# Gate and up products of a SwiGLU with the tokens stationary, and six weight sections as seven half-size products with part of their weight sums made by DMAs that add

## Chip, cores and metric

One NeuronCore of a Trainium2 chip runs one transformer-like block on 256 tokens of width 1024, in float32. The metric is the device time of one execution in microseconds (us). Engines: TensorE (PE; its weight loads are PEld), VectorE (DVE), ScalarE (ACT), GpSimd (POOL), and SyncE (SP), which only issues transfers here.

## What is computed

```python
x = x + 0.5 * rmsnorm(swiglu(rmsnorm(x, g1), W_gate1, W_up1, W_down1), p1)   # D = 1024, F = 4096
h = rmsnorm(x, gm)
q, k, v, f, u, v_s, a_A, a_B = split(h @ W_in)                               # seven sections of 1024 columns, f of 8
o_A = forgetting_attention(q, k, v, f)                                       # 8 heads of 128
o_B = gelu(u) * (W_s @ layernorm(gelu(v_s)) + b)
x = x + rmsnorm((sigmoid(a_A) * o_A + sigmoid(a_B) * o_B) @ W_out, pm)
x = x + 0.5 * rmsnorm(swiglu(rmsnorm(x, g2), W_gate2, W_up2, W_down2), p2)

def swiglu(h, w_gate, w_up, w_down):
    return (silu(h @ w_gate) * (h @ w_up)) @ w_down
```

## The kernel before, in words

Every large product runs in float32r, in three passes: an operand is cut into `hi`, its leading bits, and `lo = x - hi`; the result is hi·hi + hi·lo + lo·hi. `split` (L77) makes both parts: ACT copies `hi` (L78) and DVE subtracts (L79). The weights are split when they have come from HBM: `load` (L90) brings 1 MiB into one of 3 raw buffers from SP's queue, `piece` (L97) splits 1024 of its 2048 columns into one of 11 pairs of buffers (`wts`). The tokens are two tiles of 128; their normalised, transposed and split form stands in `xT`.

The two SwiGLUs (`ffn`, L220) go over 32 F tiles of 128 hidden columns. `gate_up` (L232) makes gate and up of one F tile with the weights stationary and the tokens moving (`wide`, L189): per 128 rows of the contraction a product of 512 columns with `hi` (L194) and one of 256 with `lo` (L195). The result comes out transposed already, as the down product needs it: `wide_sum` (L197) adds its halves, `swiglu` (L212) applies silu, multiplies and splits it into `hT`. `down` (L265) then adds this F tile into four PSUM banks, six products of 512 columns per token tile (L274). The down products of the last 10 F tiles wait for token tile 1 until tile 0 is done (`DEFER`), and two of these come after tile 0 has been put into xT (`KEEP`). The second SwiGLU starts with 4 F tiles by token tile, tokens stationary (`gate_up_of`, L240, products of 256 columns, L250), since tile 1 is not normalised yet; their results are turned by PE transposes (L260).

The mixer takes 1024 columns at a time with the tokens stationary: `proj` (L316) does 512 columns of one token tile, three products (L321) per 128 rows. `section` (L327) does both token tiles with each weight, `section_by_tile` (L341) one tile and then the other. Small work on PE is put off by some of these steps (`later` and `tick`, L118, L121). The norms are made by ACT (squares, L139), POOL (root, L144, L146) and DVE (L164, L182, L186); `to_xT` (L154) transposes on PE (L158) and splits.

The program is written without engine orders except where `in_order` (L81) sets them. The order on each engine is fixed when the program is built, by what is expected to be ready first and then by the order written; a buffer is given to the next user when its last reader is done.

Of the kernel before, what the change touches and what calls it, by code (L numbers as in the profile page):

```python
# [34 lines left out]
DEFER = 10          # last F tiles whose down product waits for token tile 1 until token tile 0 is done  # L35
KEEP = 2            # of these, the ones that come after token tile 0 is put into xT
LEAD = 4            # F tiles of the second SwiGLU that are done by token tile
WARM = 14           # idle products before the first data are there
FORGET, SCORES, TURN = 5, 3, 3  # chunks of other work before these steps (see later)
# [3 lines left out]
def block(ctx: ExitStack, tc: tile.TileContext, a: dict, out: bass.AP):  # L43
    nc = tc.nc
    const = ctx.enter_context(tc.tile_pool(name="const", bufs=1))
    raws = ctx.enter_context(tc.tile_pool(name="raws", bufs=3))
    wts = ctx.enter_context(tc.tile_pool(name="wts", bufs=11))
    gains = ctx.enter_context(tc.tile_pool(name="gains", bufs=2))
    mid = ctx.enter_context(tc.tile_pool(name="mid", bufs=12))
    big = ctx.enter_context(tc.tile_pool(name="big", bufs=3))  # L50
    small = ctx.enter_context(tc.tile_pool(name="small", bufs=4))
# [29 lines left out]
    def in_order(instructions):  # L81
        """Each engine takes its instructions of the list in the list's order."""
# [14 lines left out]
    def piece(raw, j, name, trace=None):  # L97
        r = raw[:, j * 1024:(j + 1) * 1024]
        hi = wts.tile([P, 1024], F32R, tag="hi", name=f"hi_{name}_{j}")
        lo = wts.tile([P, 1024], F32R, tag="lo", name=f"lo_{name}_{j}")  # L100
        done = split(hi, lo, r)
        if trace is not None:
            trace.extend(done)
        return hi, lo

    def unit(src, name):
        """1 MiB of weights, split into two pieces of 1024 columns."""
        raw = load(src, name)
        return [piece(raw, j, name) for j in range(2)]
# [577 lines left out]
```

## Time and profile before

| | us |
|---|---|
| median of 3 runs | 766.69 (766.54 to 766.77) |
| span of the profiled execution | 766.7 |
| PE busy | 755.1 |
| DVE busy | 486.4 |
| ACT busy | 413.2 |
| POOL busy | 17.4 |
| read from HBM | 140.02 MB, 184 GB/s over the span |

The span runs from the first to the last instruction of one execution. PE's products are pipelined, so that the duration of one overlaps the next; how fast they follow each other is read from the starts in the timeline. Idle time of an engine is put down to what released it.

### The profile page before, as it was taken

The page shows a single profiled execution, that of the slowest core. Times are in us where ns is not written, and L with a number is a line of the kernel's source. Part 1 is how long each engine was busy: PE and PEld are TensorE (multiplying, and loading weights), DVE is VectorE, ACT ScalarE, POOL GpSimd, SP SyncE. Part 2 cuts the span into 40 slices and gives each one's busy share as a digit, 9 for nine tenths or more (in the row PEclk, how much of TensorE's full clock was granted, in tenths as well). Part 3 has the DMA queues.
Part 4 walks back from the last instruction along what each step waited for, and adds up shares of the span by engine and source line. Part 5 has one row for each costly group of instructions (what it writes and reads, how often), then busy time and mean ns, then how long its engine had stood idle before and what let it go on. Part 6 is the DMA issues. An engine that isn't in the chain of part 4 may idle for free.

```text
span 766.7 us, 10137 instructions
## 1 busy us (share of the span) xinstructions
PE 755.1 (98%) x3974; PEld 641.4 (84%) x3974; DVE 486.4 (63%) x731; ACT 413.2 (54%) x655; POOL 17.4 (2%) x32
## 2 busy tenths in 40 slices
PE   7999999999999999999999999999999999999996
PEld 4888888888888878888888888898888888888885
DVE  5885665666566586755486646875666566565652
ACT  4865555554545585754544434754555555554441
POOL 1000000000000020000010000200000000000000
PEclk8999999999999999999999999999999999999999
DMA  7885455555444366633346725555455545544401
GB/s 287 309 316 222 169 215 180 205 171 215 165 165 143 136 219 221 236 136 140 115 160 196 273 84 216 196 219 217 165 194 193 205 177 194 191 167 163 165 1 55
DMA packets 21983, 141.72 MB, mean 185 GB/s; under 512 B 3184, under 2 KB 3440, under 8 KB 5680
## 3 DMA queue, kind: packets, MB, share of 16 engines
q1 hardware_dynamic: 21936, 141.08, 51.0%
q8 instruction: 31, 0.51, 0.3%
q14 instruction: 16, 0.13, 0.1%
HBM read 140.02 MB, written 1.05 MB: 184 GB/s over the span
## 4 chain that ended last, share of the span: by engine, by line
PE 97%; DMA 1%; ACT 0%; DVE 0%; POOL 0%; issue 0%; SPq 0%; DVEq 0%; POOLq 0%; ACTq 0%
PE y L274 22%; PE g L194 15%; PE u L194 14%; PE u L195 8%; PE g L195 7%; PE qk L194 4%; PE gu L250 3%; PE v L321 3%; PE ga L321 3%; PE sv L321 3%; PE wo L321 3%; PE gb L321 3%; PE u L321 3%; PE qk L195 2%; DMA g_ffn_pre_g<-in_ffn_pre_g 1%; PE tp_f L158 1%
## 5 line engine op out<-in xcount | busy, mean ns | idle before, releaser
L79 DVE TENSOR_TENSOR lo_g<-raw_g,hi_g 128x1024 fp32r<-128x1024 f32 x128 | 155.9, 1224 | 88.0 <-ACT hi_g L78 87.8
L78 ACT CAST hi_g<-raw_g 128x1024 fp32r<-128x1024 f32 x128 | 133.3, 1049 | 73.8 <-PE y L274 60.0
L194 PE MATMUL u<-xT,hi_g 128*128 128x512 f32 x480 | 171.4, 394 | 0.0
L194 PE MATMUL g<-xT,hi_g 128*128 128x512 f32 x480 | 171.2, 395 | 0.0
L274 PE MATMUL y<-hi_d,hT 128*128 128x512 f32 x512 | 148.7, 392 | 0.0
L195 PE MATMUL u<-xT,lo_g 128*128 128x256 f32 x480 | 135.9, 283 | 0.0
L195 PE MATMUL g<-xT,lo_g 128*128 128x256 f32 x480 | 135.0, 281 | 0.0
L79 DVE TENSOR_TENSOR lo_d<-raw_d,hi_d 128x1024 fp32r<-128x1024 f32 x64 | 78.1, 1225 | 48.7 <-ACT hi_d L78 48.7
L274 PEld LDWEIGHTS y<-hi_d,hT 128*128 128x128 f32 x512 | 92.1, 188 | 19.1
L194 PEld LDWEIGHTS g<-xT,hi_g 128*128 128x128 f32 x480 | 90.5, 188 | 20.7 <-ACT hi_g L78 0.3
L194 PEld LDWEIGHTS u<-xT,hi_g 128*128 128x128 f32 x480 | 90.3, 188 | 20.6
L195 PEld LDWEIGHTS g<-xT,lo_g 128*128 128x128 f32 x480 | 90.4, 188 | 3.1 <-DVE lo_g L79 0.8
L195 PEld LDWEIGHTS u<-xT,lo_g 128*128 128x128 f32 x480 | 90.2, 188 | 0.1
L274 PE MATMUL y<-lo_d,hT 128*128 128x512 f32 x256 | 80.0, 391 | 0.0
L78 ACT CAST hi_d<-raw_d 128x1024 fp32r<-128x1024 f32 x64 | 66.7, 1049 | 16.8 <-PE u L194 9.7
L201 ACT ACTIVATE low_g<-g 128x256 f32<-128x256 f32 x60 | 23.0, 383 | 72.5 <-PE g L195 72.4
L274 PEld LDWEIGHTS y<-lo_d,hT 128*128 128x128 f32 x256 | 48.1, 188 | 10.6
L204 DVE TENSOR_TENSOR s_g<-g,low_g 128x256 f32<-128x256 f32 x60 | 25.4, 424 | 33.3 <-ACT low_g L201 33.3
L78 ACT CAST hT<-s_u 128x256 fp32r<-128x256 f32 x60 | 24.1, 402 | 30.9 <-DVE s_u L217 30.8
L215 ACT ACTIVATE sg<-s_g 128x256 f32<-128x256 f32 x60 | 25.0, 417 | 27.2 <-DVE s_g L204 27.2
L79 DVE TENSOR_TENSOR hT<-s_u,hT 128x256 fp32r<-128x256 f32 x60 | 25.2, 420 | 8.4 <-ACT hT L78 8.2
L217 DVE TENSOR_TENSOR s_u<-sg,s_u 128x256 f32<-128x256 f32 x60 | 25.5, 425 | 1.9
(324 smaller groups left out, 985.7 us busy)
## 6 DMA issues: line engine op xcount, KB each, us to landing
raw_g<-in_gu SPq DMA_DIRECT2D x63, 1024.0 KB, 4.8
raw_d<-in_dn SPq DMA_DIRECT2D x32, 1024.0 KB, 4.8
x<-in_x SPq DMA_DIRECT2D x2, 512.0 KB, 3.8
raw_g<-in_gu SPq DMA_DIRECT2D x2, 512.0 KB, 8.6
g_ffn_post_g<-in_ffn_post_g SPq DMA_DIRECT2D x2, 512.0 KB, 8.8
raw_v0a<-in_w_v SPq DMA_DIRECT2D x1, 1024.0 KB, 4.7
raw_v0b<-in_w_v SPq DMA_DIRECT2D x1, 1024.0 KB, 4.8
raw_v1a<-in_w_v SPq DMA_DIRECT2D x1, 1024.0 KB, 4.8
```

Source lines behind the costliest of these rows:

```text
L78: return [nc.scalar.copy(out=hi, in_=src), nc.vector.tensor_tensor(out=lo, in0=src, in1=hi.bitcast(F32), op=ALU.subtract)]
L79: nc.vector.tensor_tensor(out=lo, in0=src, in1=hi.bitcast(F32), op=ALU.subtract)]
L158: nc.tensor.transpose(out=ps[:, i * P:(i + 1) * P], in_=src[:, i * P:(i + 1) * P], identity=ident)
L194: nc.tensor.matmul(ps, lhsT=hi, rhs=xT[:, k], start=k == 0, stop=False, skip_group_check=True)
L195: nc.tensor.matmul(top, lhsT=lo, rhs=xT[:, k, :, 0, :], start=False, stop=k == KT - 1, skip_group_check=True)
L201: nc.scalar.activation(out=low, in_=pv[:, :, 1, :], func=AF.Copy, scale=scale)
L204: nc.vector.tensor_tensor(out=s, in0=pv[:, :, 0, :], in1=low, op=ALU.add)
L215: nc.scalar.activation(out=sg, in_=g, func=AF.Silu)
L217: nc.vector.tensor_tensor(out=u, in0=sg, in1=u, op=ALU.mult)
L250: nc.tensor.matmul(ps[:, i * 256:(i + 1) * 256], lhsT=xT[:, k, t, xs, :], rhs=w, start=k == 0 and q == 0, stop=k == KT - 1 and q == 2, ski ...
L274: nc.tensor.matmul(ys[t][c], lhsT=hT[:, t, xs, :], rhs=w[:, c * 512:(c + 1) * 512], start=f == 0 and q == 0, stop=f == NF - 1 and q == 2)
L321: nc.tensor.matmul(ps, lhsT=xT[:, k, t, xs, :], rhs=w, start=k == 0 and q == 0, stop=k == KT - 1 and q == 2)
```

## The change

Gate and up are cut into four blocks of 1024 hidden columns each, gate and then up, and run like the mixer's sections with the tokens stationary: the gate of block 0 by token tile, the others with both tiles per weight. Each result [tokens, 512] goes through silu and the product as a whole and is then turned by four PE transposes (`turn` in `up_done`, two steps later) and split into hT. The down products of a block are spread over the steps of the next one; the last block's come at the end, two F tiles of the block before (`HOLD`) ahead of them.

The up sections of blocks 1 to 3 of both SwiGLUs (six of the 32 sections of 1024 columns that the kernel has) go through `fast`: of the two halves of tokens, contraction and columns it makes seven products of half size in each dimension instead of eight (Winograd's form of Strassen's method), each of 12 matmuls of 512 columns. The sums of the tokens are made once per SwiGLU (`sums`, in block 0). The sums of the weights are made in place in the raw buffers: two per section by DVE (`add`), two by a DMA from HBM that adds (`more`, issued from POOL). So a section has seven splits of 2048 columns instead of four. Five mixes on DVE (`mixed`) put the results together.

Weights are now split 2048 columns at a time (`parts_of`, `quarter`), 4 pairs of buffers of that size instead of 11 of half of it; raw buffers 5 instead of 3; work tiles (`mid`) 10 instead of 12. `KEEP` stays; `DEFER` and `LEAD` go. In the second SwiGLU token tile 1 is put into xT after the second step of the by-tile gate (`before`). The mixer's sections are the same but for the size of the splits. The flag `FASTM`, which would send mixer sections through `fast`, is empty.

```diff
-    raws = ctx.enter_context(tc.tile_pool(name="raws", bufs=3))
-    wts = ctx.enter_context(tc.tile_pool(name="wts", bufs=11))
+    raws = ctx.enter_context(tc.tile_pool(name="raws", bufs=5))
+    wts = ctx.enter_context(tc.tile_pool(name="wts", bufs=4))
...
+    def parts_of(raw, name, parts=1, trace=None):
+        hi = wts.tile([P, 2048], F32R, tag="hi", name=f"hi_{name}")
+        lo = wts.tile([P, 2048], F32R, tag="lo", name=f"lo_{name}")
+        for c in range(0, 2048, 2048 // parts):
+            cs = slice(c, c + 2048 // parts)
+            done = split(hi[:, cs], lo[:, cs], raw[:, cs])
+            if trace is not None:
+                trace.append(done)
         return hi, lo
...
+    def proj(ps, t, w, kh, i, n):
+        for k in range(i * 4 // n, (i + 1) * 4 // n):
+            hi, lo = [v[:, k * 512:(k + 1) * 512] for v in w]
+            for q, (xs, v) in enumerate(((0, hi), (0, lo), (1, hi))):
+                nc.tensor.matmul(ps, lhsT=xT[:, kh * 4 + k, t, xs, :], rhs=v, start=kh == 0 and k == 0 and q == 0,
+                                 stop=kh == 1 and k == 3 and q == 2)
...
+    def section(src, name, done):
+        for c in range(2):
+            pss = [None, None]
+            for kh in range(2):
+                w = quarter(src[c, kh], f"{name}{c}{kh}")
+                for i in range(2):
+                    for t in range(NT):
+                        if pss[t] is None:
+                            pss[t] = bank(f"{name}{t}{c}")
+                        proj(pss[t], t, w, kh, i, 2)
+                    if kh == 1 and i == 1:
+                        for t in range(NT):
+                            done(t, c, pss[t])
+                    yield
...
+    def sums(name):
+        kept = big.tile([P, NT, 2, 512], F32, tag="b", name=f"kept_{name}")
+        for t in range(NT):
+            for c in range(2):
+                hi, lo = [xT[:, c * 4:c * 4 + 4, t, i, :].bitcast(F32) for i in range(2)]
+                nc.vector.tensor_tensor(out=kept[:, t, c].rearrange("p (k c) -> p k c", c=P), in0=hi, in1=lo, op=ALU.add)
+        a11, a12, a21, a22 = [kept[:, i, j] for i in range(2) for j in range(2)]
+        parts = part.tile([P, 4, 4, 2, P], F32R, tag="p", name=f"parts_{name}")
+        v = []
+        for i, (p, q, op) in enumerate(((a21, a22, ALU.subtract), (0, a11, ALU.subtract), (a11, a21, ALU.subtract),
+                                        (a12, 1, ALU.add))):
+            p, q = [v[z] if isinstance(z, int) else z for z in (p, q)]
+            v.append(mid_tile([P, 512], f"sum_{name}{i}"))
+            nc.vector.tensor_tensor(out=v[i], in0=p, in1=q, op=op)
+            split(parts[:, i, :, 0, :], parts[:, i, :, 1, :], v[i].rearrange("p (k c) -> p k c", c=P))
+        return parts
+    def fast(src, name, parts, done):
+        def get(c, kh):
+            return load(src[c, kh], f"{name}{c}{kh}")
+        def lhs_x(kh, t):
+            return lambda k, xs: xT[:, kh * 4 + k, t, xs, :]
+        def lhs_s(i):
+            return lambda k, xs: parts[:, i, k, xs, :]
+        def product(ps, lhs, raw, nm, start):
+            w = parts_of(raw, f"{name}{nm}")
+            for k in range(4):
+                hi, lo = [z[:, k * 512:(k + 1) * 512] for z in w]
+                for q, (xs, z) in enumerate(((0, hi), (0, lo), (1, hi))):
+                    nc.tensor.matmul(ps, lhsT=lhs(k, xs), rhs=z, start=start and k == 0 and q == 0,
+                                     stop=k == 3 and q == 2, skip_group_check=True)
+        def add(out, p, q):
+            nc.vector.tensor_tensor(out=out, in0=p, in1=q, op=ALU.add)
+        def more(raw, c, kh):
+            nc.gpsimd.dma_start(out=raw, in_=src[c, kh], accum_op=ALU.add)
+        def mixed(nm, p, q, op):
+            o = mid_tile([P, 512], f"{name}{nm}")
+            nc.vector.tensor_tensor(out=o, in0=p, in1=q, op=op)
+            return o
+        b11 = get(0, 0)
+        a = bank(f"{name}A")
+        product(a, lhs_x(0, 0), b11, "p1", True)
+        p1 = mid_tile([P, 512], f"{name}p1")
+        nc.scalar.copy(out=p1, in_=a)
+        yield
+        b12 = get(1, 0)
+        add(b11, b11, b12)
+        c = bank(f"{name}C")
+        product(c, lhs_s(0), b11, "p5", True)
+        yield
+        b22 = get(1, 1)
+        more(b11, 1, 1)
+        b = bank(f"{name}B")
+        product(b, lhs_s(1), b11, "p6", True)
+        u2 = mixed("u2", b, p1, ALU.add)
+        w = mixed("w", c, u2, ALU.subtract)
+        yield
+        add(b12, b12, b22)
+        b21 = get(0, 1)
+        product(a, lhs_x(1, 0), b21, "p2", False)
+        done(0, 0, a)
+        yield
+        d = bank(f"{name}D")
+        product(d, lhs_s(2), b12, "p7", True)
+        done(1, 1, mixed("y11", w, d, ALU.subtract))
+        yield
+        product(c, lhs_s(3), b22, "p3", False)
+        done(0, 1, mixed("y01", c, u2, ALU.subtract))
+        yield
+        more(b11, 0, 1)
+        product(d, lhs_x(1, 1), b11, "p4", False)
+        done(1, 0, mixed("y10", d, u2, ALU.add))
+        yield
...
+        def gate_done(b):
+            def go(t, c, y):
+                sg = mid_tile([P, 512], f"sg{n}_{b}{t}{c}")
+                nc.scalar.activation(out=sg, in_=y, func=AF.Silu)
+                sgs[t, c] = sg
+            return go
+        def up_done(b):
+            def go(t, c, y):
+                h = sgs[t, c]
+                nc.vector.tensor_tensor(out=h, in0=y, in1=h, op=ALU.mult)
+                def turn():
+                    f4 = 2 * b + c
+                    if f4 not in hTs:
+                        hTs[f4] = big.tile([P, 4, NT, 2, P], F32R, tag="b", name=f"hT{n}_{f4}")
+                    ps = bank(f"hp{n}_{b}{t}{c}")
+                    for i in range(4):
+                        nc.tensor.transpose(out=ps[:, i * P:(i + 1) * P], in_=h[:, i * P:(i + 1) * P], identity=ident)
+                    marks[n, f4] = split(hTs[f4][:, :, t, 0, :], hTs[f4][:, :, t, 1, :],
+                                         ps.rearrange("p (i c) -> p i c", c=P))[1]
+                later(2, turn)
+            return go
+        side, parts = [], []
+        for b in range(NB):
+            steps = []
+            for src, kind, fn in ((gs[b], "g", gate_done(b)), (us[b], "u", up_done(b))):
+                nm = f"{kind}{n}_{b}"
+                if (b, kind) == (0, "g"):
+                    steps.append((section_by_tile(src, nm, fn, first), 8))
+                elif (b, kind) in quick:
+                    steps.append((fast(src, nm, parts[0], fn), 7))
                 else:
-                    late.append(nxt)
-                nxt += 1
-        late.append(NF - 1)
-        down(late[0], 1)
-        down(late[1], 1)
-        down(NF - 1, 0)
+                    steps.append((section(src, nm, fn), 8))
+            total = sum(k for _, k in steps)
+            keep = HOLD if b == NB - 1 else 0
+            had, gone, at = len(side) - keep, 0, 0
+            for gen, _ in steps:
+                for _ in gen:
+                    at += 1
+                    if b == 0 and at == 2 and before:
+                        before()
+                    if b == 0 and at == 9 and quick:
+                        parts.append(sums(f"f{n}"))
+                    tick()
+                    while had > 0 and gone < had * at // total:
+                        f = side.pop(0)
+                        down(f, 0)
+                        down(f, 1)
+                        gone += 1
+            side += range(8 * b, 8 * b + 8)
+        for f in side[:HOLD]:
+            down(f, 0)
+            down(f, 1)
+            tick()
+        late = side[HOLD:]
+        for f in late:
+            down(f, 0)
         done(0, ys[0])
-        for e in late[2:-KEEP]:
-            down(e, 1)
-        if n == 1:
-            turned(0)
+        for f in late[:-KEEP]:
+            down(f, 1)
+        if after:
+            after()
         for c in range(2):
-            for e in late[-KEEP:]:
-                down(e, 1, (c,))
+            for f in late[-KEEP:]:
+                down(f, 1, (c,))
         done(1, ys[1])
...
-    ffn(1, 0, done1, lambda t: turn[t]())
+    ffn(1, FAST1, done1, after=lambda: turn[0](), first=first)
...
-    ffn(2, LEAD, done2, lambda t: turn[t]())
+    ffn(2, FAST2, done2, before=lambda: turn[1]())
```

## Rows read from the trace of the kernel before

**Rows 1.** The page: span; busy us, share, instructions by engine.

```profile
span 766.7 us, 10137 instructions
...
PE 755.1 (98%) x3974; PEld 641.4 (84%) x3974; DVE 486.4 (63%) x731; ACT 413.2 (54%) x655; POOL 17.4 (2%) x32
```

**Rows 2.** Waits of PE, whole span: waiter, waited for; us, times, longest.

```profile
PE tp_f L158 <- DVE hn_f L164: 3.4, 1, 3.4
...
PE tp_mx L158 <- DVE hn_mx L164: 0.7, 1, 0.7
```

**Rows 3.** Windows: length; busy us of PE, PEld, DVE, ACT, POOL; clock; DMA share; GB/s.

```profile
13.70:284.40 270.70, 269.93 (x1417) 230.58 (x1417) 181.27 (x247) 158.05 (x248) 2.61 (x4) 1.00 0.56 202
...
490.90:760.40 269.50, 269.50 (x1489) 234.00 (x1487) 162.56 (x222) 138.56 (x221) 3.50 (x6) 1.00 0.48 171
```

**Rows 4.** Timeline of PE, one F tile: start, duration, work.

```profile
29.09 0.40 PE L194 MATMUL g<-xT,hi_g 128*128 128x512 f32 x1
...
34.69 0.63 PE L274 MATMUL y<-hi_d,hT 128*128 128x512 f32 x2
...
37.44 0.40 PE L194 MATMUL g<-xT,hi_g 128*128 128x512 f32 x1
```

**Rows 5.** Timeline of PE in the wo section, last quarter.

```profile
484.46 0.40 PE L321 MATMUL wo<-hi_wo1a,xT 128*128 128x512 f32 x1
...
487.24 1.04 PE L158 MATMUL tp_f<-ident,hn_f 128*128 128x128 f32 x8
...
488.03 0.48 PE L321 MATMUL wo<-hi_wo1b,xT 128*128 128x512 f32 x1
...
488.35 0.39 PE L321 MATMUL wo<-lo_wo1b,xT 128*128 128x512 f32 x1
```

**Rows 6.** Timeline of PE, first and 20th product of the lead.

```profile
490.90 0.29 PE L250 MATMUL gu<-hi_g,xT 128*128 128x256 f32 x1
...
493.18 0.28 PE L250 MATMUL gu<-lo_g,xT 128*128 128x256 f32 x1
```

**Rows 7.** Groups by line and shape: count, busy us, mean ns, idle before.

```profile
L79 DVE TENSOR_TENSOR lo_g<-raw_g,hi_g 128x1024 fp32r<-128x1024 f32 x128 | 155.9, 1224 | 88.0 <-ACT hi_g L78 87.8
...
L78 ACT CAST hi_g<-raw_g 128x1024 fp32r<-128x1024 f32 x128 | 133.3, 1049 | 73.8 <-PE y L274 60.0 <-PE u L194 10.7 <-DMA raw_g<-in_gu 1.8
...
L79 DVE TENSOR_TENSOR xT<-tp_f,xT 128x512 fp32r<-128x512 f32 x8 | 5.2, 686 | 1.7 <-ACT xT L78 1.7
...
L78 ACT CAST xT<-tp_f 128x512 fp32r<-128x512 f32 x8 | 4.4, 590 | 7.7 <-PE tp_f L158 7.7
...
L534 DVE TENSOR_TENSOR oA<-oA,sga 128x512 f32<-128x512 f32 x4 | 2.7, 689 | 1.2 <-ACT sga L533 1.2
```

**Rows 8.** The page's DMA issues, median landing; then two windows as before.

```profile
raw_g<-in_gu SPq DMA_DIRECT2D x63, 1024.0 KB, 4.8
...
6.00:16.00 10.00, 6.52 (x26) 4.83 (x24) 6.72 (x11) 4.71 (x9) 0.87 (x3) 0.66 1.00 374
...
20.00:60.00 40.00, 40.00 (x216) 34.40 (x215) 32.73 (x43) 30.06 (x45) 0.00 (x0) 1.00 0.85 315
```

**Rows 9.** Timelines of POOL and DVE between mixer and second SwiGLU.

```profile
492.22 1.23 POOL L144 TENSOR_SCALAR r_pm<-ms_pm 128x1 f32<-128x1 f32 x1 [6.73 <-ACT junk_pm L139]
...
496.55 0.30 POOL L144 TENSOR_SCALAR r_f<-ms_f 128x1 f32<-128x1 f32 x1 [2.46 <-ACT junk_f L139]
...
490.93 2.35 DVE L79 TENSOR_TENSOR lo_g<-raw_g,hi_g 128x1024 fp32r<-128x1024 f32 x2
...
497.53 1.41 DVE L164 SCALAR_TENSOR_TENSOR hn_f<-x,r_f,g_ffn_pre_g 128x512 f32<-128x512 f32 x2 [0.85 <-POOL r_f L146]
```

**Rows 10.** Timeline of PE, first products.

```profile
13.69 0.79 PE L194 MATMUL g<-xT,hi_g 128*128 128x512 f32 x1
...
14.28 0.63 PE L194 MATMUL u<-xT,hi_g 128*128 128x512 f32 x1
...
14.95 0.58 PE L195 MATMUL g<-xT,lo_g 128*128 128x256 f32 x1
```

More of the change, by code (lines that the diff above doesn't have):

```diff
@@ L95, in load, with quarter @@
         return raw
[L97 to L103, printed above, removed]
-        return hi, lo
-    def unit(src, name):
-        raw = load(src, name)
-        return [piece(raw, j, name) for j in range(2)]
-    def view(piece, **kw):
-        (k, n), = kw.items()
-        return [w.rearrange("p (k n) -> p k n", k=n) for w in piece]
+    def parts_of(raw, name, parts=1, trace=None):
[6 more added lines that the diff above has]
+                trace.append(done)
+        return hi, lo
+    def quarter(src, name):
+        return parts_of(load(src, name), name)
     pending = []
@@ new lines, in section_by_tile @@
+    def section_by_tile(src, name, done, first=None):
+        ws = {}
+        for t in range(NT):
+            for c in range(2):
+                for kh in range(2):
+                    if (c, kh) not in ws:
+                        ws[c, kh] = first if first and (c, kh) == (0, 0) else quarter(src[c, kh], f"{name}{c}{kh}")
+                ps = bank(f"{name}{t}{c}")
+                for kh in range(2):
+                    proj(ps, t, ws[c, kh], kh, 0, 1)
+                    if kh == 1:
+                        done(t, c, ps)
+                    yield
@@ L265, in down, with ffn @@
+    marks = {}
+    def ffn(n, quick, done, before=None, after=None, first=None):
+        gs, us, dn = a[f"g{n}"], a[f"u{n}"], a[f"dn{n}"]
+        hTs, ys, downs, sgs = {}, {}, {}, {}
         def down(f, t, cs=(0, 1)):
             if f not in downs:
-                downs[f], downs[f + 1] = unit(dn[f // 2], f"d{n}_{f}")
+                w = quarter(dn[f // 2], f"d{n}_{f}")
+                for i in range(2):
+                    downs[f + i] = [v[:, i * 1024:(i + 1) * 1024] for v in w]
             if t not in ys:
@@ L288, in ffn @@
-        late = []
-        nxt = 0
-        for f in range(lead, NF):
-            gate_up(f, first if (n, f) == (1, 0) else unit(gu[f], f"g{n}_{f}"))
-            if f == lead and lead:
-                turns[-1]()
-            while nxt < f:
-                down(nxt, 0)
-                if nxt < NF - DEFER:
-                    down(nxt, 1)
-                else:
-                    late.append(nxt)
-                nxt += 1
-        late.append(NF - 1)
-        down(late[0], 1)
-        down(late[1], 1)
@@ L476, in mixer, with columns @@
         kept = forget()
-        section_by_tile(a["w_v"], "v", v_done)
+        run(section_by_tile(a["w_v"], "v", v_done))
+        parts = sums("mx") if FASTM else None
+        def columns(src, name, done):
+            run(fast(src, name, parts, done) if name in FASTM else section(src, name, done))
         oA = attention(v, *kept)
-        ws = raws.tile([P, H, P], F32, tag="raw", name="ws")
+        ws = aux.tile([P, H, P], F32, tag="aux", name="ws")
         nc.vector.memset(ws[64:128, :, 0:64], 0.0)
```

153 lines of the change are left out of this document (38 added, 115 removed).

## The prediction

> **What bounds the kernel now.** I read the page's busy times first: TensorE (PE) is busy for 755.1 of 766.7 us [rows 1]. Busy PE is not yet PE at its peak, so the waits of PE come next: the only ones after the start are 3.4 us for the first normalised tile and 0.7 us at the end of the first SwiGLU [rows 2]. The windows by stage say the same: PE is busy for 269.93 of 270.70 us in the first SwiGLU and for all 269.50 us of the second, at a granted clock of 1.00 (2.4 GHz), while VectorE (DVE) works 181.27 and 162.56 us in them [rows 3]. So the time is what PE's instructions take one after the other, and what counts is the distance between their starts, which the timeline shows; the mean durations overlap and are longer.
>
> Prices on PE, from these distances. A gate/up F tile with the weights stationary takes 34.69 - 29.09 = 5.60 us, and the down product of an F tile for both token tiles 37.44 - 34.69 = 2.75 us, 12 products of 0.229 us [rows 4]. With the tokens stationary, 12 products of 512 columns take 487.24 - 484.46 = 2.78 us, 0.232 each. Eight transposes take 488.03 - 487.24 = 0.79, and the product after them starts its successor 0.32 us later instead of 0.23: 0.88 for eight, 0.11 each [rows 5]. In the by-tile lead of the second SwiGLU, 19 products of 256 columns take 493.18 - 490.90 = 2.28, 0.120 each [rows 6].
>
> **What PE gains and loses.** Removed: 60 F tiles (32 + 28) x 5.60 = 336.0 us; the lead's 4 F tiles, 192 products x 0.120 = 23.0 us, and its 8 transposes, 0.9 us. Sum 359.9. Added: 16 sections of 1024 columns. Ten go in full, 96 products x 0.232 = 22.3 us each, 223.0 together; six go as seven products of 12, 84 x 0.232 = 19.5 each, 117.0 together. New too are 128 transposes (2 SwiGLUs x 4 blocks x 2 tiles x 2 halves x 4) x 0.11 = 14.1. Sum 354.1. PE's chain is 5.8 us shorter. One part alone would lose: in the full form the 16 sections cost 356.8 + 14.1 = 370.9, 11 more than now; the seven-product form gives 6 x 2.8 = 16.8 back. The down products and the mixer's PE work stay.
>
> **DVE and ScalarE (ACT).** Prices: a split of 1024 columns takes 1.224 on DVE and 1.049 on ACT, 512 columns 0.686 and 0.590 [rows 7]. Carried on along the same line, one of 2048 takes 1.224 + 1024 x 0.00105 = 2.30 on DVE and 1.049 + 0.92 = 1.97 on ACT, one after the other 4.3 us (two short ones, 2.45 and 2.10, are the upper end). An addition or mix of 512 columns takes 0.689. Per seven-product section DVE has 7 splits (16.1), 2 additions of weights (4.6), two quarters of down weights (4.6), and 13 operations of 512 columns: five mixes, four products with the gate, four low parts of turned tiles (9.0). That is 34.3 us, beside 19.5 + 4 x 2.75 + 16 x 0.11 = 32.3 us of PE. The gate section ahead of it has 4 + 2 splits, 13.8 us, beside 22.3 + 11.0 = 33.3 of PE. So DVE lags by 2.0 us inside the fast section and has 19 to spare before it. Four buffers of split weights let it be three splits, 6.9 us, ahead. I take these sections at no stall; the cover is those three splits, and without it each costs 2.0 us. The 16 additions and splits of the token sums in block 0 are some 8 us of DVE beside a section of 22.3 us that needs 9.2: nothing.
>
> **The adding transfers.** Each fast section issues two from POOL's queue, 1 MiB each; nothing else of the section is queued on POOL behind them. The first stands between the split of product 5 and that of product 6. Time 0 is the start of the first product. A buffer is free when its products are done, so product 5 gets the one of the gate's third quarter, done at -(2.74 + 2 x 2.78 + 2.74) = -11.0. Product 1 got its buffer at -16.6 and is split at -12.3; the addition on DVE ends at -10.0, the split at -5.7. Product 6 follows product 1, product 5 and one F tile of down products, at 8.3; its split has to start by 8.3 - 4.3 = 4.0. The transfer has 9.7 us, and each microsecond over that is PE idle, six times; ACT's split of product 6 would hold up the splits and copies queued behind it. The second transfer has about 17 us.
>
> No row shows a transfer that adds. Below, it can't beat a plain load of 1 MiB, 4.8 us. Above, I let it pass the queue twice, 9.6, and wait for a whole split on DVE, 2.3: POOL's small operation took 1.23 instead of 0.30 us beside two splits of 1024 columns, and ended when they did [rows 8, 9]. That is 11.9, 2.2 too late, 13 us in six sections. I take 8.5: the DMA engines at full share move 374 GB/s, so 1 MiB is 2.8 us and the fixed part of 4.8 is 2.0; it has to read its target too, 2.0 + 2 x 2.8, and 0.9 for POOL's wait as in that row. That leaves 1.2 us and no stall. DMA in the fast section: 8 MiB plus two read again, 10.5 MB in 32.3 us, 325 GB/s; the stretch from 20 to 60 us ran at 315 GB/s with a share of 0.85 without a wait of PE [rows 2, 8].
>
> The Trainium skill (Collectives: The Full Stack, "The bandwidth ceiling: the fold count and why AG ≠ RS ≠ AR") says that a transfer that adds runs at half of a copy's rate, because it reads two sources. No run here shows it; by it the estimate is the one taken, by a copy's rate it would be 2.8 us shorter. The same skill (SBUF — State Buffer, "Who interferes with whom") speaks against this change: a DVE instruction with two SBUF inputs contends with reads by GpSimd, and a holder of the shared port blocks the other for a whole instruction. The 1.23 agrees; with a whole split of 2.30 in the way instead of the 0.9, the transfer would come to an estimated 9.9, just late.
>
> **The edges.** Start: the order of instructions is fixed at the build by when they are expected to be ready; an up product runs between two gate products there [rows 10]. The by-tile gate wants 1 MiB per 2.78 us at first and DMA delivers one per 2.8, but token tile 1 can use the same quarter; I take 0.5 us, bounds 0 and 3 (one split and a half late). Between mixer and second SwiGLU: the last wo product ends at 490.9, the normalised tile 1 at 498.95, 8.05 us later [rows 6, 9]. Its transposes stood behind 72 products of 0.120, 8.6 us; now behind 24 of 0.232, 5.6. If nothing fills it, PE loses 2.5, and up to 5 with longer splits ahead of the chain's DVE steps. The order can put other products there, as at the start: 0.5 taken. At the end of the first SwiGLU the cover is as before and a chain of seven DVE and ACT steps can meet longer splits: 0.5 more than the 0.7 now, bounds -0.7 and 2.3.
>
> Sum: the profiled execution spans 766.7 and the median of the runs is 766.69, so nothing lies around the span. 766.7 - 5.8 + 1.5 = 762.4.
>
> **Rivals.** (a) The adding transfer is late, and the kernel is slower than before. For it: the margin is 1.2 us on a price no row shows. Against: when it runs, the load buffers are full and the queue is empty. A latency of 11.9 us gives 762.4 + 6 x 2.2 = 776; it decides from 9.7 + 5.8/6 = 10.7 us, where the time passes 768.2. 0.20. (b) DVE is the bound in the fast sections, since its queue doesn't keep three splits ahead or waits for PE's partial results in between. For it: 34.3 against 32.3 us. Against: in the kernel before, ACT's splits wait 60.0 us for the down products to free buffers, so they are as far ahead as buffers allow [rows 7]. 0.5 to 2.0 us each: 765.4 to 774.4, 768 in the middle. 0.22. (c) The edges are filled and the 0.7 us goes: 766.7 - 5.8 - 0.7 = 760.2, down to 758 if the products beside lighter DVE traffic run at 0.229. 0.10. (d) The forecast, 760.8 to 765: 0.48.
>
> **How the numbers follow.** A measurement of this kernel can tell 0.2%, 1.5 us, from no change: faster is under 765.2, slower over 768.2. Faster: (d), (c), and hardly any of (b): 0.57. Same: a third of (b) and a little of (a) and (d): 0.12. Slower: the rest, 0.31. The range goes from (c) to (a) at its upper bound, which takes in (b) too: 758 to 777.
>
> **What would show it.** Right: sections of 96 products 22.3 us long on PE; the fast ones with their down products 32 to 33; PE's waits after the start under 3 us together; POOL's transfers landing within 9.7 us. Wrong for (a): PE's weight loads waiting for ACT's split of product 6, and that for a DMA. For (b): the same waits for DVE with the transfer long landed. The forecast falls if the distances between products grow, or if PE's waits pass 4 us.

## The result, and the profile after

The changed kernel takes 785.49 us (median; 784.75 to 786.53) against 766.73 for the kernel before: a ratio of 1.024, interval [1.0226, 1.0255]. It is slower by 18.8 us where 4.3 us faster was forecast, and lies 8.5 us above the upper end of the range. The profiled execution took 784.75 us and spans 783.0.

The page of the changed kernel answers [rows 1] and the first of [rows 8]:

```profile
span 783.0 us, 8505 instructions
...
PE 754.7 (96%) x3446; PEld 613.4 (78%) x3446; DVE 512.1 (65%) x504; ACT 380.7 (49%) x376; POOL 32.1 (4%) x44
...
raw_u<-in_u SPq DMA_DIRECT2D x32, 1024.0 KB, 4.8
...
raw_u<-in_u POOLq DMA_DIRECT2D x12, 1024.0 KB, 8.7
```

PE is as busy as before, 754.7 us, but its share fell from 98% to 96%: PE waits. The waits of PE, as in [rows 2] (us in total, times, longest):

```profile
PE u_3B L285 <- ACT hi_u_3p L83: 5.0, 2, 3.0
PE tp_f L160 <- DVE hn_f L166: 4.3, 2, 3.3
...
PE g L217 <- DVE lo_g L84: 2.4, 2, 1.9
PE u_3A L285 <- ACT hi_u_3p L83: 2.3, 2, 1.3
PE tp_mx L160 <- DVE hn_mx L166: 1.6, 1, 1.6
```

`u_3B` is the accumulator of product 6, and the 3 is block 3: both waits for it, one in each SwiGLU, fall in the last of the three fast sections. Of blocks 1 and 2 the whole list has one wait alone, 0.4 us at `hp` in block 1.

A wait costs more than its own length, since the products behind it can run at half clock. I therefore charge every PE instruction its price from the forecast (0.232 us for 512 columns, 0.120 for 256, 0.110 for a transpose, 0.368 for the 384 columns of the attention) and add up what the distances between starts have over that. I call this the excess: 7.7 us in the kernel before, nearly all at the start, and 31.9 in the changed one. So 24.2 us are lost, while the span grew by 16.3: at these prices PE's chain without losses is 7.9 us shorter. That figure is a count of products times their prices; run e7 below checks it by a measured span. The 24.2 us:

| where | us more than before |
|---|---|
| block 3 of the first SwiGLU | 7.0 |
| block 3 of the second SwiGLU | 5.7 |
| transposes of tile 1 ahead of the second SwiGLU | 5.1 |
| end of the first SwiGLU, tile 0 for the mixer | 1.9 |
| start, second quarter of the gate | 1.4 |
| wo section, transposes | 1.3 |
| first turned tiles of a fast section (hp) | 0.6 |
| the rest, in small pieces, the v section among them | 1.2 |

**Why block 3 and not block 2.** The timelines of one engine each, put together, block 2 first (start, duration, work, and in brackets the idle time before it and its releaser). The rows are: ACT's split of product 1, DVE's of product 5, the issue of the adding transfer, the start of the section on PE, ACT's split of product 6 (in block 3 shown as one with the two splits behind it), the first matmul of product 6, and in block 3 the next product's first matmul with its wait. The line at the end of the first view is the first transfer of block 2: its size and the time from issue to landing.

```profile
145.86 1.92 ACT L83 CAST hi_u_2p<-raw_u 128x2048 fp32r<-128x2048 f32 x1 [0.35 <-PE y L353]
...
154.67 2.28 DVE L84 TENSOR_TENSOR lo_u_2p<-raw_u,hi_u_2p 128x2048 fp32r<-128x2048 f32 x1
...
157.25 0.86 POOL L292 DMA_DIRECT2D raw_u<-in_u  x1 [52.15 <-DVE lo_u_2p L84]
...
162.32 0.40 PE L285 MATMUL u_2A<-hi_u_2p,xT 128*128 128x512 f32 x1
...
165.28 1.91 ACT L83 CAST hi_u_2p<-raw_u 128x2048 fp32r<-128x2048 f32 x1 [3.11 <-PE u_2A L285]
...
170.59 0.39 PE L285 MATMUL u_2B<-hi_u_2p,parts_f 128*128 128x512 f32 x1
...
raw_u<-in_u POOLq DMA_DIRECT2D x1, 1024.0 KB, 8.0
```

```profile
214.28 1.90 ACT L83 CAST hi_u_3p<-raw_u 128x2048 fp32r<-128x2048 f32 x1 [3.15 <-PE y L353]
...
223.08 2.28 DVE L84 TENSOR_TENSOR lo_u_3p<-raw_u,hi_u_3p 128x2048 fp32r<-128x2048 f32 x1
...
225.18 0.40 PE L285 MATMUL u_3A<-hi_u_3p,xT 128*128 128x512 f32 x1
...
225.66 0.86 POOL L292 DMA_DIRECT2D raw_u<-in_u  x1 [54.98 <-DVE lo_u_3p L84]
...
234.62 5.50 ACT L83 CAST hi_u_3p<-raw_u 128x2048 fp32r<-128x2048 f32 x3 [5.86 <-DMA raw_u<-in_u]
...
236.57 0.79 PE L285 MATMUL u_3B<-hi_u_3p,parts_f 128*128 128x512 f32 x1 [2.96 <-ACT hi_u_3p L83]
...
238.37 0.79 PE L285 MATMUL u_3A<-hi_u_3p,xT 128*128 128x512 f32 x1 [1.01 <-ACT hi_u_3p L83]
```

Count from the start of the section, as the forecast did. In block 2 product 1 gets its buffer at 145.86 - 162.32 = -16.5; product 5 is split at -5.4 (the end of DVE's part), the transfer is issued at -5.1 and lands 8.0 us later at +2.9, and ACT's split of product 6 starts at +3.0. The view names a buffer (PE u_2A) as its releaser, but buffer and transfer came within 0.1 us of each other, so about 1 us was left to the limit of +4.0 (1.2 in the forecast). In block 3 product 1 gets its buffer only at 214.28 - 225.18 = -10.9, from a down product. All that follows up to the transfer is later by the same 5.6 us: product 5 is split at +0.2, the transfer is issued at +0.5 and takes 8.9 us, and ACT's split of product 6 starts at +9.4, released by the DMA, where +4.0 was the limit. Product 6 starts at +11.4 instead of +8.3.

The code has the reason. `had = len(side) - keep` takes `HOLD` = 2 F tiles away from block 3's down products, and `gone < had * at // total` spreads what is left over 15 steps. In blocks 1 and 2 eight F tiles come after steps 2, 4, 6, 8 and so on; in block 3 six come after 3, 5, 8, 10, 13, 15. A quarter of the down weights holds its buffer for two F tiles, and in both blocks product 1 takes the buffer of the first quarter (released by PE y in both rows). It comes free after step 4 in blocks 1 and 2, after step 5 in block 3, and then one F tile fewer lies before the fast section: by the forecast's prices 2.78 + 2.75 = 5.5 us.

The windows answer [rows 3] (length; busy us of PE, PEld, DVE, ACT, POOL; granted clock; DMA share; GB/s): the fast section of block 2, the start of that of block 3, and the start of the second SwiGLU.

```profile
159.00:191.50 32.50, 32.50 (x148) 26.38 (x147) 25.74 (x19) 19.39 (x14) 0.87 (x1) 1.00 0.86 283
225.10:259.00 33.90, 29.93 (x123) 23.62 (x122) 20.85 (x17) 16.53 (x12) 1.73 (x2) 0.90 0.71 206
500.39:516.00 15.61, 12.27 (x51) 9.96 (x50) 12.29 (x15) 6.99 (x11) 4.48 (x4) 0.89 0.64 235
```

Block 2 runs at clock 1.00 (2.4 GHz) with PE busy throughout. Behind the wait in block 3 the mean is 0.90: a part ran at 1.2 GHz, with products 0.43 us apart instead of 0.23 from 239 to 243 us. That is why 4.0 us of waits there cost 7.0.

**The start of the second SwiGLU**, timelines of PE, POOL and DVE:

```profile
501.44 1.99 POOL L146 TENSOR_SCALAR r_pm<-ms_pm 128x1 f32<-128x1 f32 x1 [5.82 <-ACT junk_pm L141]
...
505.74 0.40 PE L217 MATMUL g<-hi_g,xT 128*128 128x512 f32 x1
...
508.58 1.41 DVE L166 SCALAR_TENSOR_TENSOR hn_f<-x,r_f,g_ffn_pre_g 128x512 f32<-128x512 f32 x2 [0.85 <-POOL r_f L148]
...
509.48 1.94 PE L160 MATMUL tp_f<-ident,hn_f 128*128 128x128 f32 x8 [3.34 <-DVE hn_f L166]
```

After the 24th product PE has nothing before the transposes of tile 1, and the order put nothing else there. The normalised tile comes later than in [rows 9], too: POOL's small step took 1.99 us beside a split of 2.28 us, where it took 1.23 beside splits of half the size. That split ran on DVE from 500.98 to 503.26 us, and POOL's step ended 0.17 us behind it.

### The profile page after: what moved, and what is told of

Read it like the earlier page. It is cut to its first block, busy times and chain, and to the rows that moved or that the text cites. A ratio compares the mean times of both kernels' runs of the same rounds, so it can differ in the third digit from the quotient of the medians.

```text
span 783.0 us, 8505 instructions
## 1 busy us (share of the span) xinstructions
PE 754.7 (96%) x3446; PEld 613.4 (78%) x3446; DVE 512.1 (65%) x504; ACT 380.7 (49%) x376; POOL 32.1 (4%) x44
## 5 line engine op out<-in xcount | busy, mean ns | idle before, releaser
L217 PE MATMUL g<-hi_g,xT 128*128 128x512 f32 x512 | 167.7, 398 | 0.1
L217 PEld LDWEIGHTS g<-hi_g,xT 128*128 128x128 f32 x512 | 97.2, 190 | 22.8 <-ACT hi_g L83 0.6
L84 DVE TENSOR_TENSOR lo_d<-raw_d,hi_d 128x2048 fp32r<-128x2048 f32 x32 | 73.2, 2288 | 49.8 <-ACT hi_d L83 49.8
L217 PE MATMUL g<-lo_g,xT 128*128 128x512 f32 x256 | 101.7, 397 | 2.4 <-DVE lo_g L84 2.4
L84 DVE TENSOR_TENSOR lo_g<-raw_g,hi_g 128x2048 fp32r<-128x2048 f32 (+1 forms) x33 | 73.4, 2224 | 44.8 <-ACT hi_g L83 44.8
L83 ACT CAST hi_d<-raw_d 128x2048 fp32r<-128x2048 f32 x32 | 61.1, 1909 | 38.0 <-PE g L217 8.8
L83 ACT CAST hi_g<-raw_g 128x2048 fp32r<-128x2048 f32 (+1 forms) x33 | 61.2, 1856 | 33.9 <-PE u L217 10.6
L217 PE MATMUL u<-hi_u,xT 128*128 128x512 f32 x192 | 61.7, 396 | 0.0
L217 PEld LDWEIGHTS g<-lo_g,xT 128*128 128x128 f32 x256 | 48.7, 190 | 14.2 <-DVE lo_g L84 3.3
L196 PE MATMUL qk<-xT,hi_qk 128*128 128x512 f32 x128 | 46.3, 400 | 0.0
```

The costliest lines, as they stand in the source:

```text
L83: return [nc.scalar.copy(out=hi, in_=src), nc.vector.tensor_tensor(out=lo, in0=src, in1=hi.bitcast(F32), op=ALU.subtract)]
L84: nc.vector.tensor_tensor(out=lo, in0=src, in1=hi.bitcast(F32), op=ALU.subtract)]
L196: nc.tensor.matmul(ps, lhsT=hi, rhs=xT[:, k], start=k == 0, stop=False, skip_group_check=True)
L217: nc.tensor.matmul(ps, lhsT=xT[:, kh * 4 + k, t, xs, :], rhs=v, start=kh == 0 and k == 0 and q == 0, stop=kh == 1 and k == 3 and q == 2)
```

## Experiments

Ratios are to the kernel before, run on the same chip between them. In these later runs every kernel, the one before among them, takes 1.7 to 2.5 us more than its span (the kernel before: 767.58 with a span of 765.8). Across runs I therefore compare spans; those of the kernel before lay between 764.5 and 767.4, with medians of 765.8 to 766.7 in the four groups of runs. One kernel's spans differ by up to 4 us from run to run (the changed kernel: 783.0 to 784.8, the profiled run being the fastest), so differences of a microsecond or two between single spans show little; where it matters the losses are compared by place, in the excess.

**Which cause makes block 3 late (e1).** First the spacing alone: block 3's down products at the same steps as those of the other blocks.

```diff
-            had, gone, at = len(side) - keep, 0, 0
+            had, gone, at = len(side), 0, 0
+            most = had - keep
...
-                    while had > 0 and gone < had * at // total:
+                    while gone < min(most, had * at // total):
```

> Block 3's down products are spread as in blocks 1 and 2 (one F tile after the gate's steps 2, 4, 6 and 8, then after products 5 and 2), the last two F tiles still kept for the end; nothing else is changed. Theory A (the spacing of the down products decides when product 1 gets its buffer of split weights, and with it when the first adding transfer can start): the transfer of block 3 starts some 5 us before product 1 instead of beside it, lands before product 6's split is due, and the waits of 3.0 + 1.0 and 2.0 + 1.3 us at the third product with the half clock after them go: 7.0 + 5.7 = 12.7 us, span 770 to 772, time 772 to 774. Theory B (the adding transfer is simply too slow, or the last block's traffic is too dense): the transfer takes longer than 10 us or the wait only moves; span 780 or more.

778.37 us, ratio 1.0149 [1.0102, 1.0196], span 778.0. The waits for `u_3B` and `u_3A` are gone, which shows that the spacing made them. The gain in the profiled span is only 5.0 us (the other run spans 775.2), not the 11 to 13 expected. By place, the 12.7 us of block 3 are gone, but 4.3 come back at a new wait further on in the same two sections, and 3.6 at the starts of the two SwiGLUs. PE's waits:

```profile
PE tp_f L160 <- DVE hn_f L166: 7.7, 3, 3.5
PE u_3D L285 <- DVE u_3y L296: 2.6, 2, 1.5
```

DVE's mix `u_3y`, which empties the bank of product 7, stood behind splits of 2.28 us. The 3.6 us went with the clock: in the window from 8 to 24 us, and in that from 500 to 516, the mean was 0.79, against 0.89 in both windows of the changed kernel. The edit doesn't touch these two places.

**Adding transfers against DVE (e2).** All weight sums by DVE, no adding transfer:

```diff
-        more(b11, 1, 1)
+        add(b11, b11, b22)
...
-        more(b11, 0, 1)
+        add(b11, b11, b21)
```

> No DMA adds: all four weight sums of a section are made by VectorE from the raw buffers (two more additions of 2.29 us per section, 27 us of VectorE in all), and POOL's queue issues no transfer. Theory A: block 3's third product waits for an addition of 2.3 us instead of a transfer of 8.9, so 12 of the 12.7 us there go; VectorE has 38.9 us of work in a fast section of 32.3 us of TensorE with three splits (6.9 us) of lead, so 0 to 3 us are lost per section: span 771 to 785. Theory B (VectorE is the bound of the fast sections already): each of six sections loses 4 us or more, span over 790. On the side: if the 1.7 us by which the time lies over the span comes from POOL's transfers, it goes here and time equals span within 0.3 us; if it comes from another part of the change, it stays.

771.93 us, ratio 1.0063 [1.0035, 1.009], span 769.6, a little under the 771 to 785 expected. DVE is busy for 539.2 us, 27 more, and no product of a fast section waits. So DVE is not what bounds these sections, and a sum that takes DVE 2.3 us makes product 6 ready in time even with block 3's spacing, where a transfer of 8 to 9 us does not. The edges stay: 3.3 us at the transposes, 1.6 for the mixer's tile.

**The transposes one step later (e3).**

```diff
-                    if b == 0 and at == 2 and before:
+                    if b == 0 and at == 3 and before:
```

> Token tile 1 is put into xT after the third step of the second SwiGLU's by-tile gate instead of the second, 2.8 us more of products ahead of it; nothing else is changed. Theory A (the chain of norms between mixer and second SwiGLU is 9.1 us long and had 5.6 us of cover): the wait of 3.3 us falls to 0.5 to 1 and the half clock after it goes, 4 to 5 us off the span: 778 to 779. Rival (the products that fill the gap wait for the next split anyway, or the first products of tile 1 wait in its place): less than 2 us.

783.03 us, ratio 1.0209 [1.018, 1.0239], span 781.8. The wait ahead of the second SwiGLU fell from 3.3 to 0.5 us, and the clock behind it is 1.00. But the span fell by 1.2 only (by the medians of the times 2.5), not by the 4 to 5 expected. By place, 4.3 us are gone at the transposes. At the start, which the edit doesn't touch, 2.1 came on top: a wait of 2.28 us (1.94 in the changed kernel) was followed by products at half clock in this run. Block 3 lost as much as before.

**What lies around the span (e4).** In the kernel before, one load of 4 KB was issued from POOL's queue instead of SP's, so that this queue is used at all.

```diff
-        nc.sync.dma_start(out=bs, in_=a["b_s"])
+        nc.gpsimd.dma_start(out=bs, in_=a["b_s"])
```

> The kernel before with one small load (128 x 8 numbers) issued from POOL's queue instead of SP's; nothing else is changed. Theory A (a program that issues any transfer from POOL pays a fixed price outside the span of its instructions): time minus span goes from 0.0 to about 1.7 us, the span stays within 0.3 us: time 768.4. Theory B (the 1.7 us come from the adding transfers or from their size): time and span stay together, 766.7.

768.26 us, ratio 1.0011 [0.9999, 1.0023], with a span of 766.4: 1.8 us around it. But the unchanged kernel before had the same 1.8 beside it, and so had the kernel without any adding transfer. It is no price of POOL's queue or of the change. Why the first profiled execution of the kernel before had nothing around its span stays open.

**The two terms of PE's chain (e5).** All 16 sections in full, no fast one:

```diff
-FAST1 = {(b, "u") for b in range(1, NB)}
-FAST2 = {(b, "u") for b in range(1, NB)}
+FAST1 = set()
+FAST2 = set()
```

> The changed kernel with all six fast sections in the full form (96 products instead of 84, no sums of tokens or weights, no adding transfer). A (prices right, the loss is in block 3 and at the edges): the span of the changed kernel is 783.0; six sections gain 2.8 us of PE work each, +16.8, the stalls of block 3 go, -12.7, the edges stay: span 787 (785 to 789). The full form alone should then stand 11 us plus the edges' 9 to 10 above the span of the kernel before, 765.8 in this place. B (the seven products bring less than 12 product distances each, or their DVE work is what lengthens the sections and the edges): the span falls below 783.

790.18 us, ratio 1.0292 [1.0273, 1.0311], span 788.1, within the 785 to 789 expected. The waits at the edges are all there without a fast section, so they belong to the new form of gate and up and to the larger splits: 3.3 us ahead of the second SwiGLU, lo_g 2.0, the mixer's tile 1.5, the wo section 0.9.

**The size of a split (e6).** Each split of 2048 columns as two of 1024:

```diff
-        return parts_of(load(src, name), name)
+        return parts_of(load(src, name), name, 2)
...
-            w = parts_of(raw, f"{name}{nm}")
+            w = parts_of(raw, f"{name}{nm}", 2)
```

> The changed kernel with each split of 2048 columns made as two of 1024, the pieces' size of the kernel before; nothing else is changed. A (the edges are lost to splits of 2.29 us in the way of the norms' small steps): POOL's first step of a norm is back at 1.2 us or less, the wait for the mixer's second tile falls from 1.6 to about 0.7, that in the wo section from 1.3 to under 0.5, that for lo_g at the start from 2.4 to under 1; the transposes ahead of the second SwiGLU still wait 2 to 3; block 3 of each SwiGLU still waits, some 1 us less; span 776 to 779. B (the edges are lost to the order of the work, not to the size of a split): these waits stay within 0.4 us and DVE is some 14 us busier for nothing: span 783 or more.

777.19 us, ratio 1.0121 [1.0097, 1.0145], span 775.8, 7.2 less. Its PE waits:

```profile
PE u_3C L285 <- DVE lo_u_3p L84: 3.8, 2, 3.0
...
PE tp_f L160 <- DVE hn_f L166: 2.4, 1, 2.4
PE u_3B L285 <- ACT hi_u_3p L83: 1.6, 2, 1.1
PE u_3B L285 <- DVE lo_u_3p L84: 1.5, 2, 0.8
...
PE g L217 <- DVE lo_g L84: 1.0, 2, 0.7
```

The waits for the mixer's tile, in the v section and in the wo section are gone, and that at the start fell from 2.4 to 1.0. POOL's step took 1.42 and 1.35 us here, not the 1.2 or less that was expected. Block 3 still loses 11.7 us in all: shorter splits do not repair it.

**Repairs together, on DVE's sums.** Transposes one step later, with half splits (e7) and without (e8):

> The changed kernel with the second weight sum of each fast section by an addition on DVE (no adding transfer), the transposes of tile 1 ahead of the second SwiGLU one step later, and splits in two halves. A (three separate losses that add up): span 769.6 with the sums on DVE alone, less about 4.5 at the transposes and 2 to 4 at the other edges: 761 to 764, and 1.8 more in time. B (DVE with the sums and twice the splits is the bound in the fast sections, 36 against 32 us each): six waits of 1 to 4 us for lo_u, span 768 to 775.

> As the run before it in this list but with whole splits of 2048 columns: sums on DVE and the transposes one step later. A: span 769.6 less about 4.5: 765, edges at the start, the mixer and the wo section as in the changed kernel. B (the cold stretch after the transposes only moves elsewhere): span 768 to 770.

With half splits 760.98 us, ratio 0.9917 [0.9902, 0.9932], span 758.9, below the 761 expected at the least; with whole splits 767.97, ratio 1.0003 [0.9993, 1.0013], span 766.3, between the two theories. Of the first, all waits of PE after the idle products:

```profile
PE tp_f L160 <- DMA ident<-in_ident: 3.0, 1, 3.0
PE warm L651 <- DVE zero L442: 1.2, 1, 1.2
PE g L217 <- DVE lo_g L84: 1.0, 2, 0.7
```

The first is the wait of 3.4 us in [rows 2] with another releaser, and the idle products wait in the kernel before, too. The excess is 7.9 us, that of the kernel before 7.7, and the waits are nearly the same, so the span of 758.9 is what PE's shorter chain is worth: 7.8 us less than 766.7, or 6.9 less than the 765.8 of the kernel before beside it. The size of the splits alone is worth 766.3 - 758.9 = 7.4 us between these two.

**One adding transfer at a time**, in the fastest variant: only the first sum of each section (product 6, e9), or only the second (product 4, e10).

> The fastest of the variants so far (sums on DVE, transposes one step later, half splits; span 758.9) with the first weight sum of each fast section, that of product 6, made by the adding transfer again; the second sum stays on DVE. A (the first transfer is the one that is late, and only in block 3, where product 5 gets its buffer late): waits for hi_u_3p or lo_u_3p at u_3B in block 3 of both SwiGLUs, 1 to 4 us each and a stretch at half clock behind them, none in blocks 1 and 2; span 764 to 769. B (late in every section): six such waits, span over 772. C (the transfers cost nothing by themselves): 757 to 761.

> The same fastest variant with only the second weight sum of each fast section, that of product 4, by the adding transfer. A (its 17 us of room hold in all six sections): no wait at u_3D, DVE 27 us less busy than with all sums on it (12 sums of 2.29), span 757 to 760. B (in block 3 it is late, too, as the waits at u_3D with the paced block 3 suggest): waits of 1 to 3 us at u_3C or u_3D, span 762 to 766.

The second costs nothing: 761.67 us, ratio 0.9915 [0.99, 0.993], span 758.8, and PE's waits are those of e7. The first costs 12.2 us: 773.3, ratio 1.0065 [1.005, 1.008], span 771.1, more than the 764 to 769 expected. By place, against e7, 7.0 us of it lie in block 3 and 4.8 at `hp` in blocks 1 and 2. The waits of the first:

```profile
PE hp L372 <- DVE sg L364: 3.9, 4, 1.5
...
PE u_3B L285 <- ACT hi_u_3p L83: 1.8, 2, 1.4
PE u_3B L285 <- DVE lo_u_3p L84: 1.5, 2, 0.8
PE u_3C L285 <- DVE lo_u_3p L84: 1.3, 2, 0.7
```

Product 6 waits in block 3 alone, as expected. The 3.9 us at `hp` were not. In block 1 DVE's split of product 6 starts at 98.2 us, behind the transfer, where it starts at 95.7 with both sums on DVE (e7); with the second sum still its own DVE then works without a pause until 124.3, and its products with the gate come up to 1.5 us late. So there DVE does bound the section, once its start is held up.

**All adding transfers, with the spacing repaired (e11).** The first diff, with the transposes one step later and half splits:

> The changed kernel with all adding transfers kept, block 3's down products spaced as in blocks 1 and 2, the transposes one step later, and half splits. A (the spacing of block 3 is the cause, the transfers are in time wherever the spacing is that of blocks 1 and 2): no wait at u_3B; what waits at u_3D (2.6 us with whole splits) falls with the shorter splits; span 758 to 763. B (adding transfers disturb the fast sections in other ways, too): waits at u_3B, u_3C or u_3D of over 3 us in all, span 765 or more.

761.23 us, ratio 0.9912 [0.9896, 0.9929], span 759.1, excess 8.1. Block 3 of the first SwiGLU (timelines of ACT, DVE, POOL and PE):

```profile
208.71 2.00 ACT L83 CAST hi_u_3p<-raw_u 128x1024 fp32r<-128x1024 f32 x2 [0.26 <-PE y L353]
...
216.74 2.35 DVE L84 TENSOR_TENSOR lo_u_3p<-raw_u,hi_u_3p 128x1024 fp32r<-128x1024 f32 x2
...
219.39 0.86 POOL L292 DMA_DIRECT2D raw_u<-in_u  x1 [52.90 <-DVE lo_u_3p L84]
...
225.16 0.40 PE L285 MATMUL u_3A<-hi_u_3p,xT 128*128 128x512 f32 x1
...
227.34 2.00 ACT L83 CAST hi_u_3p<-raw_u 128x1024 fp32r<-128x1024 f32 x2 [2.23 <-DMA raw_u<-in_u]
...
233.43 0.39 PE L285 MATMUL u_3B<-hi_u_3p,parts_f 128*128 128x512 f32 x1
```

Product 1 has its buffer at -16.5 again, the transfer is issued at -5.8, ACT's split starts at +2.2 and product 6 at +8.3, with no wait. The transfers take as long as ever (8.3 us median). They cost nothing once they have the room, though the split still starts the moment the transfer lands (the releaser of the row at 227.34).

**The full form with the repairs of the edges (e12)**, to have the two terms by themselves:

> The full form of all 16 sections (no fast section) with the two repairs of the edges, half splits and the transposes one step later. It measures the two terms of PE's chain by themselves. A (the prices of the prediction hold): without stalls beyond those of the kernel before it stands 8 to 11 us above that kernel's span (766 in this place), at 774 to 777, and 16 to 17 above the fast variant with the same repairs (759). B (part of the loss at the edges belongs to the full form itself): over 778. C (the seven-product form gives back less than 14): under 773.

778.85 us, ratio 1.0142 [1.0125, 1.0159], span 777.7, just above the 774 to 777 expected, with no wait of PE after the start. The full form alone costs 777.7 - 766.7 = 11.0 us; the medians of the times give 778.85 - 767.87 = 11.0, too. The fast sections give back 777.7 - 758.9 = 18.8 by the spans and 778.85 - 760.98 = 17.9 by the times; 1.2 of the 18.8 lie in the first 26 us, ahead of any fast section.

## Why the forecast was wrong, step by step

**PE's prices: right.** The product of 512 columns takes 0.232 us in the new sections and 0.229 in the down products. The full form was to cost 11 and costs 11.0; the seven products were to give back 16.8 and give 17.9 to 18.8. The chain is 6.9 to 7.9 us shorter instead of 5.8, an error of 1 to 2 us on the safe side.

**DVE and ACT: right in the sum.** A split of 2048 columns was put at 2.30 and 1.97 us and takes 2.29 and 1.91. DVE was to lag by 2.0 us in a fast section under the cover of three splits; it does so without a wait, even with 27 us more to do (e2). The fast section of block 2 with its down products is 194.19 - 162.32 = 31.87 us long, for 32.3 worked out. In the changed kernel rival (b) falls: of waits for DVE its fast sections show 0.4 us at `hp`. The cover is not large: with the split of product 6 held up and one sum more on DVE (e9), four sections wait up to 1.5 us. (By rival (b)'s own bounds the middle is 769.9, not 768; no conclusion hangs on it.)

**The adding transfer: size right, room wrong. This is the step that failed.** Taken at 8.5 us, it takes 7.8 to 9.4, median 8.7, where a plain load takes 4.8. In block 2 its course agrees with the forecast within 0.5 us at every point. But the forecast worked out one section and multiplied by six: "each microsecond over that is PE idle, six times". The diff shows `keep = HOLD if b == NB - 1 else 0`, and I didn't carry it into the room: in block 3 the room is 4.0 - 0.2 = 3.8 us instead of 9.7, and ACT's split of product 6 started at +9.4 instead of +4.0 at the latest. It fails twice, at 12.7 us in all. By the forecast's own sum that alone gives 762.4 + 12.7 = 775.1, still inside the range; it took the edges below, 11.5 us instead of 1.5, to leave it. Rival (a) put 13 us on a late transfer, so the price was nearly met, but by luck, through another mechanism: the latency it asked for, over 10.7 us, never came. e1, e9 and e11 together show it: the wait comes with the first transfer, leaves with the spacing, and the second transfer costs nothing.

The Trainium skill (Collectives: The Full Stack, "The bandwidth ceiling: the fold count and why AG ≠ RS ≠ AR") puts the reduce-scatter of a ring, whose transfers add, at half the rate of an all-gather, which copies, because an add reads two sources; it gives this for rings of three ranks and more, not for a load from HBM. Here a transfer that adds took 8.7 us and a plain load 4.8, a factor of 1.8, which is near it; how much of either is the moving of data, no run here separates.

**The wait for the mixer's tile 1 ahead of the second SwiGLU: the bound was right, the value wrong.** "If nothing fills it, PE loses 2.5, and up to 5 with longer splits" was said, and 0.5 taken, since the order can put other products there as it did at the start [rows 10]. It put none, and 5.1 us went. 3.3 us of it were the wait, the rest half clock behind it. The code writes the transposes after step 2, while the by-tile gate needs tile 1 only after step 4. One step later (e3) the wait was 0.5, and with half splits nothing (e7, e11).

**The other edges: not counted in full.** The start took 1.4 more (0.5 forecast, bound 3) and the end of the first SwiGLU 1.9 (0.5, bound 2.3). The wo section, the v section and the turned tiles, some 3 us together, were not in the sum at all. What they share is the length of the split, 2.29 us: halves take the waits for the mixer's tile, in the v and wo sections and at the turned tiles away, and more than half of that at the start (e6). For the mixer's tile and in the wo section PE waits for a norm whose small step on POOL took 1.8 us beside a split, and 0.7 us with halves (e6, e7); at the start and in the v section it waits for the split itself (lo_g, lo_v). The forecast counted the larger split as cheaper (2.30 for 2.45) and gave its length only the upper bounds of three edges.

The Trainium skill (SBUF — State Buffer, "Who interferes with whom") says that a DVE instruction with two SBUF inputs contends with POOL's reads. POOL's small step, 1.99 us beside the split of 2.28 against 1.23 in [rows 9], agrees. For the adding transfer the forecast drew from it a delay of up to a whole split. The same section doesn't say that: it infers that such an instruction leaves the writing of a transfer's descriptors alone. The trace agrees with the section: all six second transfers were issued while DVE was splitting, in 0.86 to 0.87 us, all six first ones beside an idle DVE, in 0.86 to 1.06. The second ones took longer to land, by 0.4 to 1.4 us and not by 2.3; what made them, no run here shows.

**Nothing around the span: held for one execution only.** Some 1.75 us of the result lie around the span of 783.0. In the runs made later the kernel before has them, too.

Put together: 766.7 - 7.9 + 24.2 = 783.0, against 766.7 - 5.8 + 1.5 in the forecast. The repairs don't add up singly: spacing 5.0, halves 7.2, the later transposes 1.2 us of span, 13.4 together, but all three at once 783.0 - 759.1 = 23.9. By place some 10 of the 10.5 us between them are new losses in the single runs: 4.3 at `u_3D` and 3.6 at the two starts with the spacing (e1), 2.1 at the start with the later transposes (e3). None of them is left with the halves: the excess of the first 26 us is 8.3 to 9.8 us in the six kernels with half splits and 9.9 to 12.9 in the six with whole ones.

## What to carry to other kernels

When one section's schedule is multiplied by the number of sections, check the first and the last of the loop by themselves: one term of the loop (here a held-back pair of F tiles) can move the moment at which a buffer comes free, and what hangs on that buffer moves by the same time. A long transfer in a chain costs nothing as long as the buffer at its head comes early enough, so look for the head of the chain before replacing the transfer. A longer instruction that is cheaper per element can be paid for in every short chain that has to pass it on the same engine; where cover is short, cut it in halves.

## What the hardware showed that was not expected

- A DMA from HBM that adds 1 MiB into SBUF took 7.8 to 9.4 us in the changed kernel's 12 cases; the second of a section took 0.4 to 1.4 us longer than the first in all six sections.
- What a wait of PE costs depends on what follows: at the start a wait of 1.94 us was followed by products 0.23 us apart, one of 2.28 us in another variant by products 0.43 us apart for some 3.5 us. In block 3 waits of 4.0 us cost 7.0.
- The time from the first to the last instruction and the time of the run differ by 0.0 us in the first profile of the kernel before and by 1.7 to 2.5 us in all later runs, whatever the kernel.
